# Linear attention for the sample tokens: states as the moving operand in four column groups, updates from stacked high and low parts

## The chip, the cores and the metric

The kernel runs on one core of a Trainium2 chip. The metric is the time of one execution on the device, in microseconds (us); the time before is the median of three runs. Profiles come from one further execution, recorded by the hardware profiler, and their times count from the start of the span.

## What is computed

The reference is one step of a two-layer decoder trunk for two groups of requests that share the weights: a prompt of 1024 tokens and 8 sample sequences of 8 tokens each. The first layer mixes with gated linear attention (4 heads, key width 128, value width 256), the second with sliding-window attention; each has a squared-ReLU MLP and a per-layer input embedding. The change is in the linear attention, and there in the sample sequences alone. Cut to that part, for one head:

```python
def step(state, inp):                    # a chunk: all 8 tokens of each sample sequence
    qc, kc, vc, lc = inp
    bc = jnp.cumsum(lc, axis=-2)         # log decay per token and key column
    ...
    o = einsum('bhij,bhje->bhie', attn, vc) + einsum('bhid,bhde->bhie', qc * exp(bc), state)
    last = bc[:, :, -1:, :]
    new_state = exp(last)[..., None] * state + einsum('bhjd,bhje->bhde', kc * exp(last - bc), vc)
```

For each of the 8 sequences b and each head there is a state of 128 x 256 numbers (`state_gla`). The output is the attention within the 8 tokens plus the decayed queries times the state; the new state is the decayed old one plus an outer product of the 8 tokens' keys and values.

## The kernel before, in words

Activations lie with the 1024 model columns in 8 groups of 128 partitions and all 1088 tokens (1024 prompt, then 64 sample) along the free dimension. Nearly all work is matrix products with weights, done in three matmuls: operands are split into a high part in the F32R type and a low part, and `mm3` (L163 to L165) adds high x high, high x low and low x high into one PSUM tile. Weight tiles are loaded on the SyncE queue (`load`, L77; all loads are kept in order), split by ScalarE (L139) and VectorE (L140), and used from a ring of 5 with 2 raw buffers.

The linear-attention layer (`gla_layer`) walks through the 4 heads. For each head `gla_steps` makes 9 steps: 8 chunks of 128 prompt tokens (c = 0 to 7) and one step (c = 8) for the 64 sample tokens. A step computes decays (`gla_lg`, `gla_pre`), scores by levels (`gla_scores`: one matmul a level, L524), and outputs (`gla_out`, or `gla_out_sample` for the samples). Between its pieces the driver in `gla_layer` (L322 to L334) puts the next head's projection (`gla_proj`) or, for the last head, gate products (`gla_gates`), metered by estimated cost. The order of the instructions on each engine is drawn up when the kernel is built, by priority and by estimated readiness, so pieces that stand later in the code can come earlier on an engine. PSUM tiles come from three rings: `mm` (3), `gs` (2) and `gx` (3).

In `gla_out_sample` (L566 to L591) the scores of the step lie in `pp` and `pd`, the 64 decayed keys transposed to tokens x key columns in `kt`, the decayed queries in `qe` (128 x 64), the decays of the states in `sm`, the sample tokens' values in `vs` (64 of 128 rows used, the rest zero). For each sequence b:

- `km` (L574, for two sequences at a time): `kt` masked to the 8 rows of b by `bmask`;
- the state is loaded into `s0` (a ring of 2, so the load of b waits until the state of b - 2 has been stored);
- L581: two matmuls, one for each half of the value columns, with 128 state columns as the stationary operand and the 8 queries of b as the moving one, so that 8 columns of `pi` come out for each;
- L583: one F32 matmul with `km` stationary and `vs` moving (256 columns) into `pu`;
- L584: VectorE makes the new state in place, and L585 stores it on the SyncE queue.

After the loop L588 makes the part within the sequences, ScalarE copies it out (L590) and VectorE adds `pi` (L591). `onorm` then normalises the head's outputs.

In the trace an instruction with F32 operands on TensorE has two weight loads and two matmul records (L581: 64 instructions, 128 records), called passes below; one with F32R operands has one of each.

Of the kernel before, what the change touches and what calls it, by code (L numbers as in the profile page):

```python
# [11 lines left out]
F32 = mybir.dt.float32  # L12
F32R = mybir.dt.float32r
U8 = mybir.dt.uint8
AF = mybir.ActivationFunctionType
ALU = mybir.AluOpType
# [3 lines left out]
P = 128  # L20
D = 1024
KT = D // P
SEQ = 1024
NB, NT = 8, 8
TS = NB * NT
# [6 lines left out]
DV = 256  # L32
# [6 lines left out]
R = (slice(0, 64), slice(64, 128))  # L39


def _dims(ap, dims):

    return bass.AP(tensor=ap.tensor, offset=ap.offset, ap=[list(ap.ap[0])] + [list(d) for d in dims])


class Trunk:
# [204 lines left out]
    def gla_layer(self):  # L252
        nc, I, O = self.nc, self.I, self.O
        with ExitStack() as ctx:
            ga = ctx.enter_context(self.tc.tile_pool(name="ga", bufs=1))
# [3 lines left out]
            for k in range(KT):  # L259
# [14 lines left out]
                if k == KT - 1:  # L274
                    for c0, cn in CH:
                        c = slice(c0, c0 + cn)
# [7 lines left out]
            self.load(self.wa2[:17], I["wa2"].rearrange("h r c -> r h c"))  # L284

            self.vs = ga.tile([P, DV], F32, name="vs")
            self.km = ga.tile([P, 2, P], F32, name="km")
            nc.gpsimd.memset(self.vs, 0.0)
            nc.gpsimd.memset(self.km, 0.0)
            tri = ga.tile([P, P], F32R, name="tri")  # L290
            tris = ga.tile([TS, TS], F32R, name="tris")
            tf = ga.tile([P, P], F32, tag="c128", name="tf", bufs=8)
# [7 lines left out]
            t = ga.tile([P, len(LV), P], F32, tag="E", name="masks", bufs=2).rearrange("p a b -> p (a b)")  # L300
# [2 lines left out]
            self.load(t[:TS, n:n + ns], I["msks"])  # L303
            nc.scalar.copy(msk, t[:, :n])
            nc.scalar.copy(msks, t[:TS, n:n + ns])
            bmask = ga.tile([TS, NB], F32, name="bmask")
            self.load(bmask, I["bmask"])
            og = ga.tile([P, 2], F32, name="og")
            self.load(og, I["ogain"])
            self.g = dict(tri=tri, tris=tris, msk=msk, msks=msks, bmask=bmask, og=og)  # L310
# [29 lines left out]
            o = [t for d in self.head for t in d["o"]]  # L340

            xs = []
            for k in range(KT):
                d = self.double("G3" if k < 4 else "G1")
# [166 lines left out]
    def gla_scores(self, h, c, pre):  # L511

        nc = self.nc
        E, ke, qe, sm = pre
        sample = c == 8
        w, levels = (TS, LVS) if sample else (P, LV)
        tok, qk, hw = c * P, self.head[h]["qk"], w // 2
        base = qk[:, 0, tok:tok + w]
        pp, pd = self.ps("gx"), self.ps("gx")
        for l, s in enumerate(levels):  # L520
            ev = E[:, l, :].rearrange("p (n two s) -> p n two s", two=2, s=s)
            nc.vector.tensor_tensor(ev, ev, _dims(base, ([2 * s, w // (2 * s)], [T + s, 2], [1, s])), op=ALU.mult)
            m = w - s if w - s > 64 else w
            nc.tensor.matmul(pp[:m, l * hw:(l + 1) * hw], lhsT=E[:, l, :m], rhs=ev[:, :, 1, :], start=True, stop=True)  # L524
        nc.vector.tensor_tensor(ke[:, :w], ke[:, :w], base, op=ALU.mult)
        nc.tensor.matmul(pd[:w, :w], lhsT=base, rhs=qk[:, 1, tok:tok + w], start=True, stop=True)
        nc.tensor.transpose(pd[:w, P:2 * P], in_=ke[:, :w], identity=self.ident)
        kt = self.c128("kt")
        nc.scalar.copy(kt[:w, :], pd[:w, P:2 * P])
        if c:  # L530
            nc.vector.tensor_tensor(qe[:, :w], qe[:, :w], qk[:, 1, tok:tok + w], op=ALU.mult)
        return pp, pd, kt, qe, sm
# [33 lines left out]
    def gla_out_sample(self, h, st):  # L566
        nc, ga, g, d = self.nc, self.ga, self.g, self.head[h]
        pp, pd, kt, qe, sm = st
        vs, km, o, tok = self.vs, self.km, d["o"], SEQ
        self.gla_pick(self.ats[:TS], g["msks"], pp, pd, TS, LVS)  # L570
        pi = self.ps("gx")
        for b in range(NB):
            if b % 2 == 0:
                nc.vector.tensor_tensor(km[:TS], kt[:TS, :].unsqueeze(1).broadcast_to([TS, 2, P]),  # L574
                                        g["bmask"][:, b:b + 2].unsqueeze(2).broadcast_to([TS, 2, P]), op=ALU.mult)
                pu = self.ps("gs")
            i = b % 2
            s0 = ga.tile([P, DV], F32, tag="s0", name=self.uid("s0"), bufs=2)
            self.load(s0, self.I["st0"][b, h])
            for e in range(2):  # L580
                nc.tensor.matmul(pi[:, e * TS + b * NT:e * TS + (b + 1) * NT], lhsT=s0[:, e * P:(e + 1) * P],  # L581
                                 rhs=qe[:, b * NT:(b + 1) * NT], start=True, stop=True)
            nc.tensor.matmul(pu[:, i * DV:(i + 1) * DV], lhsT=km[:, i, :], rhs=vs, start=True, stop=True)  # L583
            nc.vector.scalar_tensor_tensor(s0, s0, sm[:, b:b + 1], pu[:, i * DV:(i + 1) * DV], op0=ALU.mult, op1=ALU.add)  # L584
            nc.sync.dma_start(self.O["sts"][b, h], s0)  # L585
        po = self.ps("gx")
        for e in range(2):
            nc.tensor.matmul(po[:, e * TS:(e + 1) * TS], lhsT=vs[:, e * P:(e + 1) * P], rhs=self.ats, start=True, stop=True)  # L588
        for e in range(2):
            nc.scalar.copy(o[e][:, tok:tok + TS], po[:, e * TS:(e + 1) * TS])  # L590
            nc.vector.tensor_tensor(o[e][:, tok:tok + TS], o[e][:, tok:tok + TS], pi[:, e * TS:(e + 1) * TS], op=ALU.add)  # L591

    def onorm(self, o):
        nc, g = self.nc, self.g
# [644 lines left out]
```

## Time and profile before

| | |
|---|---|
| median of 3 runs | 2753.29 us (2752.90 to 2753.79) |
| profiled execution, its own time | 2754.8 us |
| its span | 2753.0 us |
| TensorE (PE) busy | 2720.5 us, 99% of the span |
| VectorE (DVE) busy | 1446.2 us, 53% |
| ScalarE (ACT) busy | 1057.7 us, 38% |
| sample steps of the four heads (first to last L581) | 148.8 to 449.9 us |

PE is the matmul side of TensorE and PEld its weight loads, which overlap PE. Matmuls are pipelined: the duration of one (331 ns for 362 columns) is longer than the distance from its start to the next one's start, so costs on PE are read from distances of starts. In a timeline row "x4" the first number is the start of the first of four, the second the time from there to the end of the last. In a row that groups instructions the number after the bar is busy time, then the mean in ns, then the idle time ahead of them and what ended it.

### The profile page before, as it was taken

Reading aid. Unit: us, or ns where it says so; the run is one execution under the profiler, and the core shown is the slowest. Engines: PE = TensorE matmul, PEld = TensorE weight load, DVE = VectorE, ACT = ScalarE, POOL = GpSimd, SP = SyncE. Lnnn points to the kernel's source line nnn. Section 1 sums busy time; section 2 is a strip of 40 time slices with the busy share of each in tenths; the row PEclk is TensorE's granted clock in tenths of the full one; section 3 lists DMA queues with packets and bytes.
Section 4 is the critical chain, followed back from the end, with each engine's and each line's share of the span. In section 5 each row is a group of like instructions: output and inputs, shape, how many; then the busy total and the mean of one; then the engine's idle time right before and its main releaser. Section 6 shows DMA issues by size and latency. Waiting matters only on the chain.

```text
span 2753.0 us, 43316 instructions
## 1 busy us (share of the span) xinstructions
PE 2720.5 (99%) x17265; PEld 2657.6 (97%) x17265; DVE 1446.2 (53%) x3481; ACT 1057.7 (38%) x2303; POOL 128.0 (5%) x155
## 2 busy tenths in 40 slices
PE   9999999999999999999999999999999999999997
PEld 8999999999999999999999888899999999999997
DVE  5767887443433343344755677654343333333687
ACT  5555566341221122123534666532221221222465
POOL 0000000001000000000000333200000000000000
PEclk9999999999999999999999999999999999999999
DMA  3021012321211111121122211221111111111153
GB/s 124 28 64 53 28 57 69 95 68 41 69 47 50 53 51 49 45 85 47 55 79 63 60 35 40 65 75 43 46 51 46 44 54 43 46 44 46 34 182 100
DMA packets 92704, 163.34 MB, mean 59 GB/s; under 512 B 11479, under 2 KB 30571, under 8 KB 92470
## 3 DMA queue, kind: packets, MB, share of 16 engines
q1 hardware_dynamic: 89557, 155.20, 18.6%
q10 hardware_dynamic: 1152, 4.46, 0.5%
q8 instruction: 136, 2.23, 0.3%
q0 software_dynamic: 1792, 0.92, 0.2%
q14 instruction: 67, 0.54, 0.1%
HBM read 145.94 MB, written 19.98 MB: 60 GB/s over the span
## 4 chain that ended last, share of the span: by engine, by line
PE 95%; DVE 2%; ACT 1%; DMA 1%; issue 0%; POOL 0%; DVEq 0%; SPq 0%; ACTq 0%; POOLq 0%
PE mm L163 21%; PE mm L164 21%; PE mm L165 21%; PE gx L165 7%; PE gx L164 7%; PE gx L163 7%; PE gx L524 2%; PE gx L1012 1%; PE gx L998 1%; PE gx L553 1%; PE gx L548 1%; PE gs L583 1%; PE gs L981 1%; PE gx L555 0%; PE gs L231 0%
## 5 line engine op out<-in xcount | busy, mean ns | idle before, releaser
L163 PE MATMUL mm<-G,whi 128*128 128x362 f32 (+1 forms) x3416 | 1128.8, 331 | 6.4 <-ACT G L195 6.0
L164 PE MATMUL mm<-G,whi 128*128 128x362 f32 (+1 forms) x3416 | 1127.6, 330 | 0.0
L165 PE MATMUL mm<-G,wlo 128*128 128x362 f32 (+1 forms) x3416 | 1127.3, 330 | 0.1
L163 PEld LDWEIGHTS mm<-G,whi 128*128 128x128 f32 x3416 | 642.1, 188 | 12.9 <-ACT G L195 6.4
L164 PEld LDWEIGHTS mm<-G,whi 128*128 128x128 f32 x3416 | 642.6, 188 | 3.9 <-issue 1.7
L165 PEld LDWEIGHTS mm<-G,wlo 128*128 128x128 f32 x3416 | 642.2, 188 | 3.4 <-issue 1.2
L139 ACT CAST whi<-raw 128x512 fp32r<-128x512 f32 (+1 forms) x368 | 226.4, 619 | 657.0 <-PE mm L164 618.5
L165 PE MATMUL gx<-G,wlo 128*128 128x362 f32 (+1 forms) x1048 | 344.2, 328 | 0.0
L164 PE MATMUL gx<-G,whi 128*128 128x362 f32 (+1 forms) x1048 | 343.8, 328 | 0.0
L163 PE MATMUL gx<-G,whi 128*128 128x362 f32 (+1 forms) x1048 | 343.1, 328 | 0.0
L140 DVE TENSOR_TENSOR wlo<-raw,whi 128x512 fp32r<-128x512 f32 (+1 forms) x368 | 251.9, 691 | 67.7 <-ACT whi L139 67.0
L692 DVE TENSOR_TENSOR H<-H,mm 128x364 f32<-128x364 f32 (+1 forms) x256 | 136.2, 532 | 277.2 <-PE mm L165 276.0
L681 ACT ACTIVATE tmp<-tmp 128x362 f32<-128x362 f32 (+1 forms) x192 | 97.2, 507 | 462.5 <-DVE tmp L680 457.1
L165 PEld LDWEIGHTS gx<-G,wlo 128*128 128x128 f32 x1048 | 198.0, 189 | 0.0
L163 PEld LDWEIGHTS gx<-G,whi 128*128 128x128 f32 x1048 | 197.9, 189 | 0.0
L164 PEld LDWEIGHTS gx<-G,whi 128*128 128x128 f32 x1048 | 197.7, 189 | 0.0
L683 DVE TENSOR_TENSOR G<-tmp,G 128x362 fp32r<-128x362 f32 (+1 forms) x192 | 102.9, 537 | 157.5 <-ACT G L682 157.2
L680 DVE SCALAR_TENSOR_TENSOR tmp<-mm,rb 128x364 f32<-128x364 f32 (+1 forms) x128 | 68.6, 536 | 196.4 <-PE mm L165 196.4
L692 DVE TENSOR_TENSOR H<-H,gx 128x362 f32<-128x362 f32 x128 | 68.0, 532 | 141.7 <-PE gx L165 141.7
L225 ACT ACTIVATE tmp<-H 128x362 f32<-128x362 f32 (+1 forms) x126 | 63.6, 506 | 132.6 <-DVE H L629 74.2
L682 ACT CAST G<-tmp 128x362 fp32r<-128x362 f32 (+1 forms) x192 | 95.1, 496 | 5.8
L226 DVE TENSOR_TENSOR acc<-acc,tmp 128x362 f32<-128x362 f32 (+1 forms) x126 | 67.2, 535 | 36.2 <-ACT tmp L225 35.3
(244 smaller groups left out, 3024.5 us busy)
## 6 DMA issues: line engine op xcount, KB each, us to landing
raw<-in_w_up SPq DMA_DIRECT2D x128, 256.0 KB, 2.6
raw<-in_w_down SPq DMA_DIRECT2D x128, 256.0 KB, 2.6
G<-in_w_gate SPq DMA_DIRECT2D x24, 512.0 KB, 3.9
raw<-in_w_o SPq DMA_DIRECT2D x32, 256.0 KB, 2.9
raw<-in_w_q SPq DMA_DIRECT2D x24, 256.0 KB, 3.3
x<-in_xT ACTq DMA_DIRECT2D x8, 544.0 KB
hd<-H SPq DMA_DIRECT2D x8, 544.0 KB, 2.6
x<-hd SPq DMA_DIRECT2D x8, 544.0 KB, 3.6
```

Of the source, the lines that this page charges most:

```text
L139: nc.scalar.copy(hi[:, s], raw[:, s])
L140: nc.vector.tensor_tensor(lo[:, s], raw[:, s], hi[:, s].bitcast(F32), op=ALU.subtract)
L163: mm(out, lhsT=w[0], rhs=x[0], start=first, stop=False)
L164: mm(out, lhsT=w[0], rhs=x[1], start=False, stop=False)
L165: mm(out, lhsT=w[1], rhs=x[0], start=False, stop=last)
L225: nc.scalar.activation(sq[:, :cn], h[:, s], AF.Square)
L226: nc.vector.tensor_tensor(self.acc[:, s], self.acc[:, s], sq[:, :cn], op=ALU.add)
L680: nc.vector.scalar_tensor_tensor(t[:, :cn], ps, 0.0, rb[:, s], op0=ALU.max, op1=ALU.mult)
L681: nc.scalar.activation(t[:, :cn], t[:, :cn], AF.Square)
L682: nc.scalar.copy(u[:, 0, s], t[:, :cn])
L683: nc.vector.tensor_tensor(u[:, 1, s], t[:, :cn], u[:, 0, s].bitcast(F32), op=ALU.subtract)
L692: nc.vector.tensor_tensor(h[:, s], h[:, s], ps, op=ALU.add)
```

## The change

- The state is no longer the stationary operand. For each sequence the 32 query columns of its group of four (`qe[:, half*32:half*32+32]`) are stationary, and the state's 256 columns stream past them; the result goes to partitions 32i to 32i+31 of `pi`, i = b mod 4, and columns 0 to 255 or 256 to 511 for the first and the last four sequences. Of the 32 rows of each result only the 8 of sequence b are used. So there are 8 F32 matmuls for each head, on four column groups of the array, in place of 16.
- `pi` now has tokens in its partitions. ScalarE copies its two halves out (`it`), four transposes on TensorE turn them back (`pt`, a further `gx` tile), and the addition at the end picks each sequence's 8 columns.
- The update of the state uses F32R: values and keys are split into high and low parts; `k2` has the high parts of the keys in rows 0 to 63 and the low parts in rows 64 to 127, `v2[:, 0]` the high part of the values in both halves of the rows, `v2[:, 1]` their low part in both. Two F32R matmuls (`km[:, b]` against `v2[:, 0]`, then `v2[:, 1]`) take the place of one F32 matmul. `km` holds all 8 sequences, masked in one VectorE instruction; the mask `bmask` is loaded into both halves of the rows.
- `s0` has a ring of 8 instead of 2, and the 8 loads stand at the head of the function.
- In `gla_scores`, at the prompt chunks, the level s = 64 takes 65 columns of the stationary operand instead of 128 (`max(w - s, 65)`); the other levels and the sample step are as before.

```diff
@@ -284,9 +284,7 @@
             self.load(self.wa2[:17], I["wa2"].rearrange("h r c -> r h c"))
 
             self.vs = ga.tile([P, DV], F32, name="vs")
-            self.km = ga.tile([P, 2, P], F32, name="km")
             nc.gpsimd.memset(self.vs, 0.0)
-            nc.gpsimd.memset(self.km, 0.0)
             tri = ga.tile([P, P], F32R, name="tri")
             tris = ga.tile([TS, TS], F32R, name="tris")
             tf = ga.tile([P, P], F32, tag="c128", name="tf", bufs=8)
@@ -303,8 +301,9 @@
             self.load(t[:TS, n:n + ns], I["msks"])
             nc.scalar.copy(msk, t[:, :n])
             nc.scalar.copy(msks, t[:TS, n:n + ns])
-            bmask = ga.tile([TS, NB], F32, name="bmask")
-            self.load(bmask, I["bmask"])
+            bmask = ga.tile([P, NB], F32, name="bmask")
+            for r in R:
+                self.load(bmask[r], I["bmask"])
             og = ga.tile([P, 2], F32, name="og")
             self.load(og, I["ogain"])
             self.g = dict(tri=tri, tris=tris, msk=msk, msks=msks, bmask=bmask, og=og)
@@ -520,7 +519,7 @@
         for l, s in enumerate(levels):
             ev = E[:, l, :].rearrange("p (n two s) -> p n two s", two=2, s=s)
             nc.vector.tensor_tensor(ev, ev, _dims(base, ([2 * s, w // (2 * s)], [T + s, 2], [1, s])), op=ALU.mult)
-            m = w - s if w - s > 64 else w
+            m = w if sample else max(w - s, 65)
             nc.tensor.matmul(pp[:m, l * hw:(l + 1) * hw], lhsT=E[:, l, :m], rhs=ev[:, :, 1, :], start=True, stop=True)
         nc.vector.tensor_tensor(ke[:, :w], ke[:, :w], base, op=ALU.mult)
         nc.tensor.matmul(pd[:w, :w], lhsT=base, rhs=qk[:, 1, tok:tok + w], start=True, stop=True)
     def gla_out_sample(self, h, st):
         nc, ga, g, d = self.nc, self.ga, self.g, self.head[h]
         pp, pd, kt, qe, sm = st
-        vs, km, o, tok = self.vs, self.km, d["o"], SEQ
+        vs, o, tok = self.vs, d["o"], SEQ
+        s0 = []
+        for b in range(NB):
+            s0.append(ga.tile([P, DV], F32, tag="s0", name=self.uid("s0"), bufs=NB))
+            self.load(s0[b], self.I["st0"][b, h])
+
+        v2 = ga.tile([P, 2, DV], F32R, tag="v2", name=self.uid("v2"), bufs=1)
+        k2 = self.c128("k2").bitcast(F32R)
+        nc.scalar.copy(v2[R[0], 0, :], vs[R[0]])
+        nc.scalar.copy(v2[R[1], 0, :], vs[R[0]])
+        nc.scalar.copy(k2[R[0]], kt[R[0], :])
+        for r in R:
+            nc.vector.tensor_tensor(v2[r, 1, :], vs[R[0]], v2[R[0], 0, :].bitcast(F32), op=ALU.subtract)
+        nc.vector.tensor_tensor(k2[R[1]], kt[R[0], :], k2[R[0]].bitcast(F32), op=ALU.subtract)
         self.gla_pick(self.ats[:TS], g["msks"], pp, pd, TS, LVS)
+
         pi = self.ps("gx")
         for b in range(NB):
+            i, half = b % 4, b // 4
+            nc.tensor.matmul(pi[32 * i:32 * i + 32, half * DV:(half + 1) * DV], lhsT=qe[:, half * 32:half * 32 + 32],
+                             rhs=s0[b], start=True, stop=True)
+        it = [self.t364() for _ in range(2)]
+        for half in range(2):
+            nc.scalar.copy(it[half][:, :DV], pi[:, half * DV:(half + 1) * DV])
+        km = ga.tile([P, NB, P], F32R, tag="km", name=self.uid("km"), bufs=1)
+        nc.vector.tensor_tensor(km, k2.bitcast(F32).unsqueeze(1).broadcast_to([P, NB, P]),
+                                g["bmask"].unsqueeze(2).broadcast_to([P, NB, P]), op=ALU.mult)
+        for b in range(NB):
             if b % 2 == 0:
-                nc.vector.tensor_tensor(km[:TS], kt[:TS, :].unsqueeze(1).broadcast_to([TS, 2, P]),
-                                        g["bmask"][:, b:b + 2].unsqueeze(2).broadcast_to([TS, 2, P]), op=ALU.mult)
                 pu = self.ps("gs")
-            i = b % 2
-            s0 = ga.tile([P, DV], F32, tag="s0", name=self.uid("s0"), bufs=2)
-            self.load(s0, self.I["st0"][b, h])
-            for e in range(2):
-                nc.tensor.matmul(pi[:, e * TS + b * NT:e * TS + (b + 1) * NT], lhsT=s0[:, e * P:(e + 1) * P],
-                                 rhs=qe[:, b * NT:(b + 1) * NT], start=True, stop=True)
-            nc.tensor.matmul(pu[:, i * DV:(i + 1) * DV], lhsT=km[:, i, :], rhs=vs, start=True, stop=True)
-            nc.vector.scalar_tensor_tensor(s0, s0, sm[:, b:b + 1], pu[:, i * DV:(i + 1) * DV], op0=ALU.mult, op1=ALU.add)
-            nc.sync.dma_start(self.O["sts"][b, h], s0)
-        po = self.ps("gx")
+            out = pu[:, (b % 2) * DV:(b % 2 + 1) * DV]
+            for i in range(2):
+                nc.tensor.matmul(out, lhsT=km[:, b, :], rhs=v2[:, i, :], start=(i == 0), stop=(i == 1))
+            nc.vector.scalar_tensor_tensor(s0[b], s0[b], sm[:, b:b + 1], out, op0=ALU.mult, op1=ALU.add)
+            nc.sync.dma_start(self.O["sts"][b, h], s0[b])
+        po, pt = self.ps("gx"), self.ps("gx")
         for e in range(2):
             nc.tensor.matmul(po[:, e * TS:(e + 1) * TS], lhsT=vs[:, e * P:(e + 1) * P], rhs=self.ats, start=True, stop=True)
         for e in range(2):
+            for half in range(2):
+                c = (e * 2 + half) * P
+                nc.tensor.transpose(pt[:, c:c + P], in_=it[half][:, e * P:(e + 1) * P], identity=self.ident)
+        for e in range(2):
             nc.scalar.copy(o[e][:, tok:tok + TS], po[:, e * TS:(e + 1) * TS])
-            nc.vector.tensor_tensor(o[e][:, tok:tok + TS], o[e][:, tok:tok + TS], pi[:, e * TS:(e + 1) * TS], op=ALU.add)
+            dst = o[e][:, tok:tok + TS].rearrange("p (a b t) -> p a b t", a=2, b=4)
+            src = _dims(pt[:, e * 2 * P:], ([P, 2], [32 + NT, 4], [1, NT]))
+            nc.vector.tensor_tensor(dst, dst, src, op=ALU.add)
```

## Prediction

> **What bounds the kernel now.** I read the page first (busy time, slices, chain), then busy time by stretch around the linear attention, then the waits, then the order of time around one sample step.
>
> ```profile
> span 2753.0 us, 43316 instructions
> PE 2720.5 (99%) x17265; PEld 2657.6 (97%) x17265; DVE 1446.2 (53%) x3481; ACT 1057.7 (38%) x2303; POOL 128.0 (5%) x155
> PEclk9999999999999999999999999999999999999999
> PE 95%; DVE 2%; ACT 1%; DMA 1%; issue 0%; POOL 0%; DVEq 0%; SPq 0%; ACTq 0%; POOLq 0%
> ```
>
> PE is busy 99% of the span at its full granted clock, and the chain that ended last is 95% PE. That is an average; what counts is the stage that is changed. Busy time there:
>
> ```profile
> 146.00:480.00 334.00, 332.29 (x2335) 317.69 (x2334) 255.32 (x878) 195.23 (x470) 2.84 (x5) 1.00 0.18 55
> 175.00:235.00 60.00, 59.72 (x464) 57.14 (x463) 50.35 (x205) 39.77 (x114) 0.00 (x0) 1.00 0.11 32
> 235.00:270.00 35.00, 35.00 (x241) 33.85 (x240) 23.33 (x72) 13.03 (x34) 0.00 (x0) 1.00 0.28 87
> ```
>
> The columns are stretch, length, then busy time of PE, PEld, DVE, ACT and POOL. From the first sample step to the end of the layer PE is idle for 334.00 - 332.29 = 1.7 us; DVE has 255 of 334 us. In 235 to 270, around the second head's sample step, PE has no gap at all and DVE is busy for 67%. So time taken off PE here should come off the end, as long as no other chain takes its place. The waits say the same:
>
> ```profile
> PE gx L581 <- DMA s<-in_st: 0.7, 1, 0.7
> PEld gx L581 <- DMA s<-in_st: 1.2, 2, 1.0
> DVE s L584 <- PE gx L581: 18.8, 12, 3.7
> ```
>
> The two-deep ring of states makes DVE wait 18.8 us for L581, and the step drags on; PE itself waits for states only 0.7 + 1.2 us, because other matmuls are put between. A deeper ring by itself is worth no more than that. What counts is the PE time of the instructions.
>
> **What goes from PE.** One pair of sequences in the second head's sample step, matmuls and then weight loads, and the counts:
>
> ```profile
> 240.98 0.51 PE L581 MATMUL gx<-qe,s 128*128 128x8 f32 x4
> 241.34 0.68 PE L583 MATMUL gs<-vs,km 128*128 128x256 f32 x2
> 241.86 0.51 PE L581 MATMUL gx<-qe,s 128*128 128x8 f32 x4
> ...
> 240.86 0.53 PEld L581 LDWEIGHTS gx<-qe,s 128*128 128x128 f32 x4
> ...
> L581 PEld LDWEIGHTS gx<-qe,s x128: 186/191/192, 148.8 to 449.9; 128*128 128x128 f32 x128
> L581 PE MATMUL gx<-qe,s x128: 170/256/277, 148.9 to 449.9; 128*128 128x8 f32 x128
> L583 PE MATMUL gs<-vs,km x64: 377/378/462, 149.2 to 449.1; 128*128 128x256 f32 x64
> ```
>
> Four weight loads of L581 take 0.53 us in all and the last 0.19, so they start (0.53 - 0.19) / 3 = 0.113 us apart: with 8 moving columns a pass costs its weight load. From the first L581 to the next sequence's L581 are 0.88 us for four such passes and two of L583, so L583 costs (0.88 - 4 x 0.113) / 2 = 0.214 a pass. L581 in all: 128 x 0.113 = 14.5 us. L583: 64 x 0.214 = 13.7 us. Both go.
>
> The 65 columns at level s = 64 of the prompt chunks:
>
> ```profile
> L524 PE MATMUL gx<-E 128*128 128x64 f32 x64 | 12.1, 271 | 0.0
> L524 PEld LDWEIGHTS gx<-E x472: 132/188/196, 75.3 to 427.4; 128*127 128x127 f32 x22, 128*120 128x120 f32 x22, 128*128 128x128 f32 x22, 128*126 128x126 f32 x21
> 237.73 0.42 PEld L524 LDWEIGHTS gx<-E 128*64 128x64 f32 x6
> ```
>
> 64 passes have 128 stationary columns and 64 moving ones. At 64 stationary columns six loads start (0.42 - 0.13) / 5 = 0.058 us apart. I take 0.058 for 65 columns, half of 0.113 as the columns are. Saved: 64 x (0.113 - 0.058) = 3.5 us. The bounds are 0 (the load isn't what limits it) and 3.5.
>
> **What comes to PE.** The update in F32R, 8 x 2 x 4 = 64 passes with 256 moving columns. The same shape in the value projection, the first and the last of 15 in a row:
>
> ```profile
> 142.57 0.27 PE L163 MATMUL mm<-whi,G 128*128 128x256 f32 x1
> ...
> 144.23 0.28 PE L165 MATMUL mm<-whi,G 128*128 128x256 f32 x1
> ```
>
> That is 1.66 / 14 = 0.119 us a pass, and 64 x 0.119 = 7.6 us.
>
> The states as moving operand: 8 F32 matmuls a head with 32 stationary and 256 moving columns, 16 passes. The kernel has four column groups of 32 elsewhere, in the sample tokens' window attention:
>
> ```profile
> 1626.85 1.09 PE L998 MATMUL gx<-ident,S 128*128 128x128 f32 x8
> 1627.87 0.42 PE L1031 MATMUL gs<-kp,qs 64*32 64x128 f32 x8
> 1628.22 0.43 PE L1033 MATMUL gs<-Ks,qs 64*128 64x64 f32 x2
> L998 PE MATMUL gx<-ident,S 128*128 128x128 f32 x240 | 38.8, 287 | 4.2 <-DVE S L963 3.1 <-POOL S L963 0.3
> ```
>
> Eight passes of 128 columns in four groups start and end within 0.42 us; one after the other their columns alone would take 8 x 0.107 (half of L583's pass). So four run side by side. The last L998 starts at 1626.85 + 1.09 - 0.29 = 1627.65, the next full-width instruction at 1628.22: 0.57 us, less one L998 pass (0.114, below) and two rounds of 0.107, leaves 0.24 for going into the mode, spreading the groups, and coming out. A head then costs four rounds of 0.214 and 0.24, 1.1 us; the four heads 4.4 us.
>
> This is a drain on a change of mode, as the Trainium skill states it ("TensorEngine Tiling (Array Packing)", Key Properties); the rows agree, and give it the size of 0.24 us for the way in and out.
>
> What the rows don't show is four groups with 128 rows each: L1031 has 64. Bounds: side by side as in L1031 (4.4 us), or 16 passes in a row, 16 x 0.214 + 0.24 = 3.7 us a head, 14.7 us. I take the first, the nearest row in shape, and keep both.
>
> Transposes back, 4 a head of 128 columns: eight of L998 start (1.09 - 0.29) / 7 = 0.114 us apart; 16 x 0.114 = 1.8 us.
>
> The Trainium skill speaks against these ("TensorE: Matmul & The Clock Gate", Part 4): about 275 ns for a transpose in a kernel's context. By that they would take 16 x 0.275 = 4.4 us and the gain would be 2.6 us smaller, an estimate; the L998 row disagrees, since there 0.287 is the length of one and not its distance from the next.
>
> **The sum for PE.** Off: 14.5 + 13.7 + 3.5 = 31.7. On: 7.6 + 4.4 + 1.8 = 13.8. Net 17.9 us less.
>
> **What the other engines get.** The rows for their new work:
>
> ```profile
> L574 DVE TENSOR_TENSOR km<-kt,bmask 64x256 f32<-64x256 f32 x16 | 6.6, 414 | 5.1 <-PE gs L583 4.3 <-ACT kt L529 0.8
> L193 DVE TENSOR_TENSOR G<-H,G 128x1088 fp32r<-128x1088 f32 x22 | 28.1, 1288 | 9.4 <-ACT G L192 9.3
> L525 DVE TENSOR_TENSOR ke<-ke,G 128x128 f32<-128x128 f32 x32 | 9.2, 286 | 0.0
> L466 ACT CAST lgh<-lge 128x256 fp32r<-128x256 f32 x16 | 6.3, 396 | 0.7 <-DVE lge L465 0.7
> L392 ACT ACTIVATE G<-mm,rt 128x256 f32<-128x256 f32 x32 | 15.1, 471 | 23.9 <-PE mm L165 23.7
> ```
>
> DVE, a head: `km` with 1024 columns 1024/1088 x 1.288 = 1.21, two differences for `v2` at 0.414, one for `k2` at 0.286, together 2.3 in place of 4 x 0.414 = 1.7: 0.6 us more. ACT: three copies for the splits at no more than 0.396 and two of `pi` at 0.471, 2.1 us more. In 235 to 270 DVE has 11.7 us free and ACT 22, so I cost both at nothing. Without that cover the way from `kt` to the first update is what shows: a copy of at most 0.396, a difference of 0.286 and 1.21 for the mask, 1.9 us, against 0.414 before, 1.5 us a head.
>
> Behind it on the in-order PE queue stand that head's updates and whatever the build put after them; behind the long `km` on DVE the next head's score products. The extra `gx` tile and the new order of stores get no price of their own; a rival takes the first. The loads:
>
> ```profile
> 109.82 0.90 SPq L77 DMA_DIRECT2D s<-in_st  x2
> DMA to landing us min/median/max: 2.0/2.3/2.8
> L77 SPq DMA_DIRECT2D s<-in_st x32: 333/366/426, 109.8 to 446.3; - x32
> ```
>
> SP issued the first two states at 109.8, 39 us before the first L581 (148.8). Now all eight can go then, 8 x 0.43 = 3.4 us of queue, with weight loads behind them. A weight tile feeds 36 matmuls of 362 columns, over 36 x 0.119 = 4.3 us, and three are kept ahead, so I cost this at nothing; uncovered it is 3.4 us a head. The second small load of `bmask` lies ahead of the sample steps: nothing.
>
> **From the span to the time.** 2753.0 - 17.9 = 2735.1 for the span. The profiled execution took 2754.8, 1.8 more than its span and 1.5 more than the median of the three runs. So 2735.1 + 1.8 - 1.5 = 2735.4 against a median of 2753.29. A measurement of this kernel tells some 0.2%, 5.5 us, from no change.
>
> **The rivals.**
>
> - *PE waits at each sample step*, for the split and the mask (1.5 us a head) or for weights (up to 3.4): 4 x 1.5 = 6.0 gives 2741.4; up to 2749.0 for the weights. For: DVE's queue is a shared one. Against: PE waits for DVE hardly at all now, with DVE slower to its first update than PE could be. 0.13.
> - *The groups run in a row, or at half speed*, since four streams of 128 rows are read at once. Half speed costs 4 x 4 x 0.214 = 3.4, 2738.8; in a row 14.7 - 4.4 = 10.3, 2745.7. Against: L1031's rows. 0.12, mostly for half speed.
> - *The visits are split* (the one without a measurable gain). If the eight matmuls of a head are placed one by one between other work, as each state lands, each costs two passes and the change of mode, 2 x 0.214 + 0.24 = 0.67; 32 of them are 21.4 in place of 4.4, and 0.9 us of gain is left: 2752.4. For: the build does put other matmuls between L581 now. Against: it does so because of the ring of two; with eight buffers the states can be there 39 us early. 0.04. The drain named above is what makes this dear.
> - *Slower: the next head's first step starves.* `po` and `pt` take two of the three `gx` tiles until the last additions, and the next step's `pp` and `pd` need two. If that step waits, and with it the chain of DVE work behind it, PE works off the projections and then stands idle for up to a step. A step is (240.98 - 148.8) / 9 = 10.2 us; at three joints 30.7, so 2735.4 + 30.7 = 2766.1. It decides from (17.9 + 5.5) / 3 = 7.8 us a joint. Against: now `pi` alone holds a tile through the whole loop, and PE loses 1.7 us in 334. 0.03.
> - *The 65 columns bring nothing*: 2738.9. Against: the 0.058 above. 0.03.
>
> **How the numbers follow.** The forecast, all terms within a microsecond or two, has 0.65; the rivals 0.35. Faster by over 0.2% needs a time below 2747.8: the forecast, the columns, the groups, and nearly all of the waits, 0.92. Within 0.2%: the split visits and the rest, 0.05. Slower: 0.03. The range goes down by the idle 1.7 us and as much again for the drains (2732) and up to the waits at 1.5 us a head (2741.4), which takes in half speed and the columns: 2732 to 2742. In it lie the forecast, half of the waits, half speed and the columns, about 0.84.
>
> **What would show it.** Right: L581's line as 64 passes of 128*32, four starting within some 0.02 us and the rounds 0.21 apart, one visit a head; L583's line as 64 passes 0.12 apart; L524 without 128*128 at the prompt chunks but with 128*65, loads 0.06 apart; PE still without gaps from 146 to the end of the layer, and that end some 18 us earlier. Wrong: rounds 0.4 apart or more (half speed), several visits a head, PE idle for over 1 us ahead of an update or of the next head's scores, or a later stage that takes longer than before.

## The result, and the profile after

| | before | after |
|---|---|---|
| median | 2753.54 us (4 runs, 2752.90 to 2754.47) | 2739.61 us (4 runs, 2738.03 to 2741.02) |
| ratio | | 0.9948, 95% interval 0.9936 to 0.9959 |
| profiled execution, its own time | 2754.8 us | 2741.02 us |
| its span | 2753.0 us | 2738.9 us |

The change takes off 13.9 us by the medians and 14.1 by the spans. The forecast was 17.9. The lines shift: the level matmuls are now L523 (524 before), `gla_out`'s L552 and L554 (553 and 555); in `gla_out_sample` the states are L587, the updates L600, the transposes L609.

The page of the kernel after, the same rows as those shown of before:

```profile
span 2738.9 us, 43239 instructions
PE 2706.5 (99%) x17217; PEld 2639.3 (96%) x17217; DVE 1448.5 (53%) x3481; ACT 1065.8 (39%) x2326; POOL 128.0 (5%) x154
PEclk9999999999999999999999999999999999999999
PE 96%; DVE 2%; ACT 1%; issue 0%; DMA 0%; POOL 0%; DVEq 0%; SPq 0%; ACTq 0%; POOLq 0%
```

PE is busy 14.0 us less (2720.5 - 2706.5), and the span is 14.1 shorter: PE was the bound and still is.

Busy time by stretch, after (stretch, length, then PE, PEld, DVE, ACT, POOL, then the granted clock):

```profile
146.00:480.00 334.00, 332.14 (x2369) 313.67 (x2368) 265.42 (x885) 210.40 (x499) 2.84 (x5) 1.00 0.19 59
235.00:270.00 35.00, 34.96 (x241) 32.19 (x234) 32.63 (x105) 22.11 (x57) 0.00 (x0) 1.00 0.24 76
```

PE is as full as before. DVE went from 23.33 to 32.63 of the 35 us around the second sample step, ACT from 13.03 to 22.11. Most of that is work that now falls into this stretch: in the whole kernel DVE is busy only 2.3 us more (1448.5 against 1446.2) and ACT 8.1, of which 3.8 are three further loads of function tables (below). The cover under which the new work was costed at nothing is nearly used up there (2.4 us are left on DVE), but it held.

The order of time around the first sample step, and the groups of its new lines (duration min/median/max, first and last start):

```profile
147.39 0.28 PE L165 MATMUL mm<-whi,G 128*64 128x256 f32 x1
147.60 1.07 PE L587 MATMUL gx<-s,qe 128*32 128x256 f32 x16
148.60 0.32 PE L605 MATMUL gx<-ats,vs 128*128 128x64 f32 x1
```

```profile
L587 PEld LDWEIGHTS gx<-s,qe x64: 106/110/111, 147.6 to 409.6; 128*32 128x32 f32 x64
L587 PE MATMUL gx<-s,qe x64: 378/379/404, 147.6 to 409.8; 128*32 128x256 f32 x64
...
L600 PE MATMUL gs<-v,km x64: 277/282/388, 150.1 to 418.6; 128*128 128x256 f32 x64
```

All 16 passes of a head are one visit (a run of small matmuls between two of the projections) of 148.60 - 147.60 = 1.0 us, and so in all four heads. In the records they start four at a time within 0.02 us, the rounds at 147.60, 147.84, 148.06 and 148.27.

To place the difference I put the matmuls of L163 to L165 in order of their starts, the same 14,544 in both kernels, and compare the times of those with the same number. From the 400th (about 74 us) to the 2000th (about the end of the linear attention) the kernel before takes 400.9 us and the kernel after 385.8. This stretch is called the stage below. From there to the 8000th both take 1004.4 us. In the next thousand, the window attention, after takes 330.8 and before 329.3. So the stage gave 15.1 us, and 1.5 were lost where nothing was changed. That loss shows as clock:

The window attention by stretch, before:

```profile
1708.00:1712.00 4.00, 3.94 (x26) 3.65 (x26) 4.00 (x15) 2.14 (x11) 0.99 (x1) 1.00 0.00 0
...
1726.00:1734.00 8.00, 7.74 (x63) 6.09 (x59) 5.42 (x26) 4.11 (x16) 1.78 (x2) 0.70 0.00 0
```

The same, after:

```profile
1708.00:1712.00 4.00, 3.43 (x26) 2.86 (x25) 3.23 (x16) 1.39 (x4) 1.04 (x1) 0.61 0.00 2
...
1719.00:1726.00 7.00, 6.90 (x45) 5.28 (x47) 3.74 (x17) 3.14 (x10) 0.98 (x1) 0.51 0.00 0
```

The granted clock halves for pieces of 3.4 us: 6.8 us in all before (from 1724.0), 3.4 and 6.8 after (from 1708.8 and 1719.1). One piece costs up to 1.7 us, as passes then take about twice as long. The Trainium skill ("TensorE: Matmul & The Clock Gate", Part 1) tells of free-running windows of 3413 ns after which the clock is set to full or half; the pieces in these traces, 3.4 us or twice that, agree.

So the stage itself fell short of the forecast by 2.8 us (17.9 - 15.1). There is a candidate for that. The waits of PE in the linear attention, after, and its order of time at the longest:

```profile
PE gx L552 <- DVE at L540: 1.8, 3, 1.4
PE gx L523 <- DVE E L521: 0.2, 1, 0.2
```

```profile
391.39 0.32 PE L165 MATMUL mm<-G,wlo 128*128 128x362 f32 x1
393.09 0.49 PE L552 MATMUL gx<-at,G 128*128 128x128 f32 x2 [1.38 <-DVE at L540]
```

From start to start that is 1.70 us in place of 0.165. ScalarE in the time before it, after:

```profile
383.12 1.28 ACT L416 ACT_TABLE_LOAD   x1
...
386.73 1.28 ACT L463 ACT_TABLE_LOAD   x1
388.03 0.31 ACT L463 ACTIVATE lge<-lge 64x128 f32<-64x128 f32 x1
388.24 0.19 ACT L502 ACTIVATE sm<-bc 128x1 f32<-128x1 f32 x1
388.45 1.28 ACT L503 ACT_TABLE_LOAD   x1
389.74 0.20 ACT L503 ACTIVATE sm<-bc 128x1 f32<-128x1 f32 x1
389.96 1.28 ACT L107 ACT_TABLE_LOAD   x1
391.26 0.95 ACT L491 ACTIVATE E<-E 128x896 f32<-128x896 f32 x1
392.11 0.39 ACT L504 ACTIVATE ke<-bc,sm 128x128 f32<-128x128 f32 x1
```

In the order that the build drew up for the changed kernel, L463 and L503 stand between the Silu of L416 and the preload at L107. So the whole kernel has 28 table loads in place of 25, and `ke` is late. Against this candidate: the kernel before has waits too, only spread out. Its list for the stage adds up to 1.8 us (0.7 for a state, 0.4, 0.3, 0.2, 0.2), that of after to 2.0.

### The profile page after: what moved, and what is told of

Same layout as the page of the kernel before. It is cut to its first block, busy times and chain, and to the rows that moved or that the text cites. A ratio compares the mean times of both kernels' runs of the same rounds, so it can differ in the third digit from the quotient of the medians.

```text
span 2738.9 us, 43239 instructions
## 1 busy us (share of the span) xinstructions
PE 2706.5 (99%) x17217; PEld 2639.3 (96%) x17217; DVE 1448.5 (53%) x3481; ACT 1065.8 (39%) x2326; POOL 128.0 (5%) x154
## 4 chain that ended last, share of the span: by engine, by line
PE 96%; DVE 2%; ACT 1%; issue 0%; DMA 0%; POOL 0%; DVEq 0%; SPq 0%; ACTq 0%; POOLq 0%
PE mm L163 22%; PE mm L164 22%; PE mm L165 22%; PE gx L165 7%; PE gx L164 7%; PE gx L163 7%; PE gx L523 2%; PE gx L1035 1%; PE gx L1021 1%; PE gx L552 1%; PE gx L547 1%; PE gs L1004 1%; PE gs L231 0%; PE gx L554 0%; PE gs L1005 0%
## 5 line engine op out<-in xcount | busy, mean ns | idle before, releaser
L163 PE MATMUL mm<-G,whi 128*128 128x362 f32 (+1 forms) x3416 | 1129.3, 331 | 6.2 <-ACT G L195 6.2
L165 PE MATMUL mm<-G,wlo 128*128 128x362 f32 (+1 forms) x3416 | 1127.7, 330 | 0.1
L163 PEld LDWEIGHTS mm<-G,whi 128*128 128x128 f32 x3416 | 642.9, 188 | 12.7 <-ACT G L195 6.6
L165 PEld LDWEIGHTS mm<-G,wlo 128*128 128x128 f32 x3416 | 642.6, 188 | 3.2 <-issue 1.6
L165 PE MATMUL gx<-G,wlo 128*128 128x362 f32 (+1 forms) x1048 | 344.3, 329 | 0.0
L163 PE MATMUL gx<-G,whi 128*128 128x362 f32 (+1 forms) x1048 | 343.1, 328 | 0.0
L165 PEld LDWEIGHTS gx<-G,wlo 128*128 128x128 f32 x1048 | 198.0, 189 | 0.0
L163 PEld LDWEIGHTS gx<-G,whi 128*128 128x128 f32 x1048 | 197.8, 189 | 0.0
```

Of the source, the lines that this page charges most:

```text
L163: mm(out, lhsT=w[0], rhs=x[0], start=first, stop=False)
L165: mm(out, lhsT=w[1], rhs=x[0], start=False, stop=last)
```

## The theories

**First theory.** The passes cost what the forecast says and they add; what is missing went to waits and halved clocks, which come from the order of instructions that each build draws up. **Rival.** One of the terms is mis-sized (the column groups, the update or the 65 columns), and the parts done alone show which.

## Experiments

The numbers of all of them first. "Stage" is the stretch defined above, "waits" the sum of PE's waits in it that the profile lists, "half clock" the time in it at a granted clock of 0.5, all in the profiled execution. "Rest" is the stage less the waits and less half of the half clock, so about the passes alone.

| kernel | median us | ratio to before, 95% interval | stage | waits | half clock | rest |
|---|---|---|---|---|---|---|
| before | 2754.0 | | 400.9 | 1.8 | 0 | 399.1 |
| after, again (r_after) | 2740.13 | 0.9946 (0.9932 to 0.9959) | 385.8 | 2.0 | 0 | 383.8 |
| p1_cols | 2751.13 | 0.9985 (0.9976 to 0.9994) | 397.4 | 1.5 | 0 | 395.9 |
| p2_ring | 2762.55 | 1.0033 (1.0020 to 1.0045) | 409.0 | 2.2 | 13.6 | 400.0 |
| p3_groups | 2751.00 | 0.9986 (0.9977 to 0.9995) | 397.4 | 3.1 | 0 | 394.3 |
| p4_update | 2763.25 | 1.0029 (1.0018 to 1.0040) | 410.6 | 8.2 | 13.6 | 395.6 |
| q_apart | 2757.72 | 1.0009 (1.0000 to 1.0018) | 402.2 | 0.7 | 0 | 401.5 |
| q_serial | 2739.93 | 0.9943 (0.9931 to 0.9956) | 385.9 | 2.0 | 0 | 383.9 |
| q_table | 2737.88 | 0.9940 (0.9928 to 0.9953) | 385.7 | 1.1 | 0 | 384.6 |
| u_cols | 2742.12 | 0.9957 (0.9945 to 0.9969) | 388.4 | 2.1 | 0 | 386.3 |
| u_groups | 2756.30 | 1.0009 (1.0001 to 1.0017) | 406.0 | 2.8 | 27.2 | 389.6 |
| u_update | 2748.21 | 0.9980 (0.9971 to 0.9989) | 395.5 | 2.9 | 3.4 | 390.9 |

### One part alone, on the kernel before

p1_cols: the 65 columns only.

```diff
-            m = w - s if w - s > 64 else w
+            m = w if sample else max(w - s, 65)
```

> The kernel before with the 65 columns at level s = 64 alone. Theory A (each part is worth the TensorE passes that it saves, less what TensorE waits in the order that this build gives it; a half-clock window of 3.4 us more or less moves a run by 1.5 us): 64 weight loads from 0.113 to 0.058 us apart, 3.5 us less, so about 2750.0 against 2753.5, and the linear-attention stage shorter by 3.5 us. Theory B (the sum of 17.9 us was short because a term was mis-sized): if it is this term, no change within 1 us.

The stage went from 400.9 to 397.4, the 3.5 us forecast. Single runs lie between 2746.81 and 2753.92; the profiled one, 2746.81, has a full clock all through the window attention (the stretch 1719 to 1726 has 1.00), which explains its place at the low end.

p2_ring: the ring of eight and the loads ahead, nothing else.

```diff
+        s0 = []
+        for b in range(NB):
+            s0.append(ga.tile([P, DV], F32, tag="s0", name=self.uid("s0"), bufs=NB))
+            self.load(s0[b], self.I["st0"][b, h])
...
-            s0 = ga.tile([P, DV], F32, tag="s0", name=self.uid("s0"), bufs=2)
-            self.load(s0, self.I["st0"][b, h])
```

> The kernel before with eight buffers for the states and the eight loads at the head of the function, nothing else. Theory A: TensorE waited 1.9 us for states in all, so 0 to 1.9 us less, 2751.6 to 2753.5; VectorE's wait of 18.8 us for L581 shrinks to a few us, and the sample step of a head takes under 12 us in place of 24, with no gain from that. Theory B: as the step is shortened by over 10 us a head, some of that shows, over 4 us less.

It is 8.6 us slower. The order of time on PE in p2_ring (its state matmuls are L583, its updates L585), then two stretches of it:

```profile
150.17 3.19 PE L583 MATMUL gx<-qe,s 128*128 128x8 f32 x28
153.22 0.64 PE L590 MATMUL gx<-ats,vs 128*128 128x64 f32 x4
...
155.46 0.51 PE L163 MATMUL mm<-G,whi 128*128 128x364 f32 x1
155.76 0.50 PE L164 MATMUL mm<-G,whi 128*128 128x364 f32 x1
...
431.92 3.63 PE L583 MATMUL gx<-qe,s 128*128 128x8 f32 x32
435.40 0.41 PE L164 MATMUL mm<-G,whi 128*128 128x364 f32 x1
```

```profile
150.00:153.90 3.90, 3.90 (x35) 3.87 (x34) 0.73 (x3) 0.96 (x2) 0.00 (x0) 0.99 0.57 168
153.90:157.30 3.40, 3.40 (x11) 3.12 (x11) 1.79 (x7) 2.19 (x5) 0.00 (x0) 0.51 0.11 39
```

With all eight states at hand, 28 passes of 8 moving columns run back to back. PE reads as busy for 3.90 of 3.90 us and PEld for 3.87. Then the clock is halved: passes of 364 columns start 0.30 apart in place of 0.165, and 3.4 us hold 11 matmul records in place of 28 (the same stretch of before). This comes at three of the four heads, 13.6 us in all, worth up to 6.8. The fourth head has 32 such passes in a row, from 431.92, and the clock stayed at full behind them; what sets it apart is not shown.

p3_groups: the ring, the column groups and the transposes; update and 128 columns as before.

```diff
         pi = self.ps("gx")
         for b in range(NB):
+            i, half = b % 4, b // 4
+            nc.tensor.matmul(pi[32 * i:32 * i + 32, half * DV:(half + 1) * DV], lhsT=qe[:, half * 32:half * 32 + 32],
+                             rhs=s0[b], start=True, stop=True)
+        it = [self.t364() for _ in range(2)]
+        for half in range(2):
+            nc.scalar.copy(it[half][:, :DV], pi[:, half * DV:(half + 1) * DV])
```

> The kernel before with the ring of eight, the states as moving operand in four column groups, and the transposes back; update and levels as before. Theory A: 14.5 off, 4.4 and 1.8 on, 8.3 us less, 2745.2, up to 1.9 lower with the waits for states gone. Theory B: if the groups are the mis-sized term, 4 us less or under, 2749.5 or more.

Only 3.0 us by the medians, 4.8 in the rest, where the passes alone give 14.5 - 4.4 - 1.8 = 8.3: the median is where the rival put it. No half clock in the stage, but a wait that is 0.2 us at the longest in the kernel before and that the kernel after does not have:

```profile
PE gs L481 <- ACT lgh L466: 2.0, 2, 1.8
```

Here too it stands behind table loads on ScalarE (five of 1.28 us between 350 and 360 us; 29 in the kernel).

p4_update: the stacked update in F32R only, with the ring of two.

```diff
+        km = ga.tile([P, NB, P], F32R, tag="km", name=self.uid("km"), bufs=1)
...
-            nc.tensor.matmul(pu[:, i * DV:(i + 1) * DV], lhsT=km[:, i, :], rhs=vs, start=True, stop=True)
+            for i in range(2):
+                nc.tensor.matmul(out, lhsT=km[:, b, :], rhs=v2[:, i, :], start=(i == 0), stop=(i == 1))
```

> The kernel before with the update in stacked high and low parts alone; ring of two and stationary states as before. Theory A: 13.7 off and 7.6 on, 6.1 us less, 2747.4. Theory B: if the update is the mis-sized term, because its longer chain on ScalarE and VectorE holds up TensorE, 3 us less or under, 2750.5 or more, with waits ahead of L583's successor of 0.5 us or more a head.

It is 9.3 us slower though its passes are 6.1 us cheaper. The waits of PE in p4_update, and its clock behind one of them:

```profile
PE mm L163 <- ACT whi L139: 2.8, 2, 1.8
PE gx L589 <- DMA s<-in_st: 2.6, 4, 1.4
PE gs L593 <- DVE s L594: 1.8, 2, 1.3
```

```profile
358.00:361.00 3.00, 0.96 (x7) 0.77 (x7) 2.33 (x6) 2.75 (x7) 0.00 (x0) 0.93 0.74 205
361.00:364.00 3.00, 2.68 (x9) 2.42 (x9) 2.87 (x7) 0.88 (x2) 0.00 (x0) 0.50 0.18 64
```

8.2 us of waits with the small ones, and 13.6 us at half clock, 6.8 from 360.6 and 6.8 from 463.0, both beside idle times of 1.3 to 1.8 us. The parts alone sum to 2.8 + 3.0 - 9.3 = -3.5, a loss; the whole gains 14. So a part alone does not size a term. In the rest they give 3.2, 4.8 and 3.5 us, 11.5 together, against 15.3 of the whole by the same measure and 17.9 by the forecast: less than forecast for each, which speaks for the rival, though no one term stands out.

### What the halved clock needs

q_apart: p2_ring, with the state matmuls of a sequence ordered behind the update of the one before.

```diff
+                if b:
+                    self.order(r.ins, mu.ins)
-            nc.tensor.matmul(pu[:, i * DV:(i + 1) * DV], lhsT=km[:, i, :], rhs=vs, start=True, stop=True)
+            mu = nc.tensor.matmul(pu[:, i * DV:(i + 1) * DV], lhsT=km[:, i, :], rhs=vs, start=True, stop=True)
```

> The kernel with only the ring of eight states and the loads ahead, with one thing more: the state matmuls of a sequence wait for the update matmul of the sequence before it, so that they don't run back to back. No work is left out. If the 8.6 us that the ring alone cost come from the run of weight loads with 8 moving columns each, after which the granted clock is halved for 3.4 to 6.8 us, there is no stretch at half clock in the sample steps of the linear attention and the kernel falls back to 2754 to 2757 us, within 3 us of the kernel before. If they come from waits and table loads of the other build order, it stays at 2760 to 2763 us.

The same stretch as in p2_ring, in q_apart:

```profile
153.90:157.30 3.40, 3.40 (x31) 3.29 (x29) 2.89 (x10) 0.00 (x0) 0.00 (x0) 1.00 0.25 86
```

No half clock in any sample step, and the stage falls from 409.0 to 402.2: 6.8 us, half of the 13.6. The median, 2757.72, is 0.7 us above the range expected and 3.7 above before; of that the stage holds 1.3. So the halving in the sample steps hangs on the run of passes with 8 columns; the matmuls are the same in number and shape. That a run is not always enough, p2_ring's fourth head shows.

### One part undone, on the kernel after

u_cols: 128 columns again (p1_cols' edit, reversed).

> The changed kernel with one part undone: the level s = 64 takes 128 columns again. If the terms of the forecast add once the rest is in place, the linear attention takes 3.5 us more (385.8 to 389.3 us between the two marks used for the stage) and the kernel 2743.6 us. If each build's own order of instructions moves the time by as much as a part is worth, the stage comes out anywhere from 386 to 393 us, with the difference in idle time of TensorE or in how the small matmuls are split up between the projections.

The stage grew by 2.6 us, the rest by 2.5 and the median by 2.0 (against 2740.13), where 3.5 were expected. PE's wait ahead of L552 is there as in after.

u_groups: the states stationary again, no transposes; ring, stacked update and 65 columns stay.

```diff
-            i, half = b % 4, b // 4
-            nc.tensor.matmul(pi[32 * i:32 * i + 32, half * DV:(half + 1) * DV], lhsT=qe[:, half * 32:half * 32 + 32],
-                             rhs=s0[b], start=True, stop=True)
...
+            for e in range(2):
+                nc.tensor.matmul(pi[:, e * TS + b * NT:e * TS + (b + 1) * NT], lhsT=s0[b][:, e * P:(e + 1) * P],
+                                 rhs=qe[:, b * NT:(b + 1) * NT], start=True, stop=True)
```

> The changed kernel with one part undone: the states are the stationary operand again, 16 F32 matmuls of 8 moving columns a head and no transposes; ring of eight, stacked update and 65 columns stay. By the passes alone 14.5 less 4.4 less 1.8, 8.3 us more (stage 394.1, kernel 2748.4). If a run of weight loads with 8 moving columns each halves the granted clock after it, as with the ring alone, there are stretches at half clock of 3.4 to 6.8 us behind the sample steps, and up to 1.7 us more for each 3.4 us of them: stage 396 to 402, kernel 2750 to 2757. If that halving belonged to something else in the ring's build, no such stretch shows in the sample steps and the stage is at 394 to 395.

16.2 us slower than after, and 2.3 slower than before. PE around the first sample step of u_groups, and the stretch behind:

```profile
148.70 3.63 PE L587 MATMUL gx<-qe,s 128*128 128x8 f32 x32
152.19 0.64 PE L602 MATMUL gx<-ats,vs 128*128 128x64 f32 x4
...
153.89 0.51 PE L163 MATMUL mm<-G,whi 128*128 128x364 f32 x1
```

```profile
153.90:157.30 3.40, 3.40 (x17) 3.40 (x17) 1.36 (x4) 1.64 (x6) 0.00 (x0) 0.55 0.12 39
```

Half clock behind all four sample steps (20.4 us), and 6.8 us more behind PE's wait of 2.4 us for ScalarE (L480, to 365.7). The stage, 406.0, lies above the 396 to 402 expected. The rest is 5.8 us over after's, where the passes alone give 8.3. So of 20.2 us of stage most is clock, up to 13.6. The profiled execution is the slowest of twelve (2762.52), but the clock shows in the others too: the one with a mean granted clock of 0.996, as before the change, took 2749.37, near the 2748.4 of the passes alone, and the other eleven, at 0.991 to 0.994, took 2755.60 to 2762.52. In the whole change the column groups are worth twice what their passes say.

u_update: the single F32 update again; ring, groups and 65 columns stay.

```diff
-            for i in range(2):
-                nc.tensor.matmul(out, lhsT=km[:, b, :], rhs=v2[:, i, :], start=(i == 0), stop=(i == 1))
+            nc.tensor.matmul(pu[:, i * DV:(i + 1) * DV], lhsT=km[:, i, :], rhs=vs, start=True, stop=True)
```

> The changed kernel with one part undone: the update of the states is one F32 matmul of 256 columns against km of 64 rows again, with km masked for two sequences at a time; ring of eight, column groups and 65 columns stay. By the passes alone 13.7 less 7.6, 6.1 us more (stage 391.9, kernel 2746.2). The same kernel without the 65 columns had its stage at 397.4, so 393.9 if the columns add. If the stage lies between 391 and 394.5 the terms hold to some 2 us; further off, the build's own order weighs as much as the part.

8.1 us slower than after, the stage 9.7 longer and 1.0 above the range expected. It has 3.4 us at half clock, behind PE's longest wait:

```profile
355.00:359.50 4.50, 2.67 (x18) 2.37 (x17) 3.31 (x12) 4.29 (x11) 0.00 (x0) 0.99 0.00 0
359.50:362.90 3.40, 3.40 (x14) 3.40 (x13) 2.58 (x11) 3.34 (x7) 0.00 (x0) 0.51 0.01 2
```

The rest is 7.1 us over after's, against 6.1 by the passes. p3_groups and u_update differ by the 65 columns alone and have the same wait ahead of L481: 394.3 - 390.9 = 3.4. Behind that wait the clock stayed at full in p3_groups.

So from the top the terms are 2.5 of 3.5 (u_cols), 5.8 of 8.3 and 7.1 of 6.1, 15.4 of 17.9 together: what the whole gave. The mechanism of the first theory, waits and half clocks, explains most of what p4_update and u_groups are off by; of the 5.3 us that p3_groups is off it covers 1.3. For the whole's missing 2.8 us it falls: after has no more waits than before (2.0 us against 1.8) and no half clock in the stage. There the rival is nearer. The states' matmuls fall shortest, 4.8 from below and 5.8 from above where 8.3 were worked out; but the rest of each build also holds what its order of instructions makes of the other passes, so the parts do not settle which price was off; the stages of before and after, shared out among their passes, say more (below).

### The column groups and the table loads

q_serial: the sequences in the order 0, 4, 1, 5, 2, 6, 3, 7, so that two matmuls of one group follow each other.

```diff
-        for b in range(NB):
+        for b in (0, 4, 1, 5, 2, 6, 3, 7):
             i, half = b % 4, b // 4
```

> The changed kernel, but the eight sequences are built in the order 0, 4, 1, 5, 2, 6, 3, 7, so that two matmuls of the same column group follow each other. No work is left out. If a column group's second pass holds up the other groups behind it (the queue is strictly in order), a head of sample tokens takes some 13 rounds of 0.22 us in place of four: 9 times 0.215 us more, 1.9 us a head, 7.7 us for four heads (about 2747). If the four groups take their passes from the queue independently, as the first profile hints where the first passes of all four groups start ahead of every second pass, four rounds stay and the time is the changed kernel's within 0.5 us.

The first sample step of q_serial:

```profile
147.88 1.09 PE L587 MATMUL gx<-s,qe 128*32 128x256 f32 x16
148.90 0.66 PE L605 MATMUL gx<-ats,vs 128*128 128x64 f32 x4
```

1.02 us against 1.00, four rounds, in all four heads, and the stage unchanged at 385.9. The built program does hold the two matmuls of a group next to each other on PE. Passes of a group that is free start ahead of earlier ones that wait for a group that is busy. The Trainium skill says that matmuls stay in program order and only weight loads are pulled ahead ("TensorE: Matmul & The Clock Gate", Part 2); for passes on different column groups the runs disagree, as 16 passes in this order would need some 13 rounds.

r_after: the kernel after, once more.

> The changed kernel once more. The first theory (passes add as forecast, part of it is lost to waits of the new build order and to 3.4 us stretches at half clock that fall into the window attention in some executions) expects a median of 2739.6 us within 1.5, the linear attention up to its last matmul at 385 to 386 us again, the 1.7 us gap of TensorE near 391 us again since it comes from the order of the instructions, and single runs that differ by multiples of some 1.5 to 2 us. The rival (the 1.7 us gap and the half clock stretches of the first profile are chance) expects that the gap is gone in the second profile and the median nearer to 2736.

The stage is 385.8 us again and the wait at L552 is there again, now 392.84 us after the span's start. It belongs to the order of the instructions. The window attention took 329.3 us, as before the change, and the profiled execution 2738.2 us; so the 1.5 us there come and go from one execution to the next. The median stayed at 2740.13.

q_table: the Exp and Ln of the layer ordered behind the table preload, each Silu behind the last of them.

```diff
+    def tabled(self, r):
+        if getattr(self, "lastpre", None) is not None:
+            self.order(r.ins, self.lastpre)
+        self.lastexp = r.ins
+        return r
...
+            self.order(self.lastsilu.ins, self.lastexp)
...
-            nc.scalar.activation(sm[:, 0:1], bc[:, P - 1:P], AF.Exp, scale=1.0 / 16)
+            self.tabled(nc.scalar.activation(sm[:, 0:1], bc[:, P - 1:P], AF.Exp, scale=1.0 / 16))
```

> The changed kernel with one thing more: on ScalarE each Exp and Ln of the linear attention comes after the table preload ahead of it, and each Silu after the last of them, so that the 28 table loads become 25 as in the kernel before. No work is left out. If the three loads of 1.28 us between a Silu and the preload are what delays ke and starves TensorE at 391 us, the 1.7 us gap there goes and the kernel takes 1.4 to 1.7 us less than the changed kernel (about 2738.0). If the gap belongs to something else (VectorE's splits ahead of it), the loads go and the time stays within 0.5 us of the changed kernel. If the added order makes ScalarE late elsewhere, it is slower by 1 us or more.

The 28 loads became 25, and of PE's waits between 380 and 400 us only this is left in q_table:

```profile
PE gx L555 <- ACT kt L536: 0.2, 1, 0.2
```

So the table loads did make the wait. But the stage is 385.7 us, no shorter than in after: the rest grew by as much as the waits fell. The small matmuls lie differently there (they interrupt the projections 167 times in place of 162); that the gain was spent in this is likely and not shown. The median of 2737.88 is lower, but the five runs (2736.19 to 2741.25) overlap with those of r_after (2738.20 to 2740.76); no gain is shown, and no kernel tried is shown to beat the kernel after.

## Why the prediction was right, and where it was off

The time lies in the range and on the side that had 0.92. By its steps:

- **PE bounds the stage, so its time comes off the end.** Right: 14.0 us less busy time, 14.1 us less span, and the matmuls behind the stage keep their distances.
- **Column groups on.** Right: one visit a head, rounds of about 0.22 us, 1.0 us a visit against 1.1. Groups with 128 rows run side by side at the full rate, which the rows of before did not show. Half speed and groups in a row are out.
- **L581 and L583 off.** This is where the sum was too large. The 0.113 and 0.214 us were read from one pair of sequences in which L581 and L583 follow each other; elsewhere they lie between projections. The stage can be shared out whole: to each pass the distance from its start to the next start, less idle time. By this L581 has 11.9 us and L583 11.0 in the kernel before, 22.9 in place of 28.2. Where each distance is charged to the later pass instead, they have 27.4. So the term was 1 to 5 us too large; neighbours share the rest, and no run here parts it further.
- **F32R and transposes on.** By the first way of sharing, the updates have 8.6 us in the kernel after, the groups 4.0 and the transposes 1.3: 13.9 in place of 13.8 (15.8 by the second way). In the order of time three transposes start within 0.22 us, 0.11 apart. Each of the 16 has one record, not two, and it lasts 0.272 us, near the 275 ns that the Trainium skill states ("TensorE: Matmul & The Clock Gate", Part 4); that is the length of one and not its price here.
- **A part that no term had.** Off, on and 3.5 us for the levels make 12.5 of the 15.1 us by the first way. The other 2.6 are 2.9 less in passes that the change does not touch, 2.4 of it in the projections (254.9 us before, 252.5 after), and 0.3 more idle time. By the second way the projections lose 2.5. Why they became cheaper is open. So that the sum came so near the measured time is luck in part: a price that was too high, and a gain that nobody had worked out.
- **The 65 columns.** 3.5 in the stage when done alone, 2.6 when undone from the whole, against the 3.5 worked out.
- **"I cost both at nothing".** Held in sum: the waits of PE are 2.0 us against 1.8. Their place is new. The rival of PE waiting came true not at the update of a sample step but ahead of a prompt chunk's outputs (L552), through table loads that no term had, and the waits for states are gone.
- **"A deeper ring by itself is worth no more than that."** Wrong in sign: alone it cost 8.6 us, mostly since it lets weight loads run in a row and the clock is halved behind them (q_apart, without such runs, has 6.8 us less of stage). The change escapes because the column groups replace those passes; without them it would have been 2.3 us slower than the kernel before (u_groups).
- **From the span to the time.** Single executions move by some 3 us with the pieces at half clock in the window attention, which the working did not have. They are likely the other part of the 4.2 us between 2735.4 and 2739.61.

## What to carry to other kernels

Where one engine is 99% busy, a sum of its passes by distances of starts gave the side and most of the size here, with some luck; read the price of a pass at several places, since neighbours share it. Do not size the parts of a change by running each alone: here they sum to a loss of 3.5 us where the whole gains 14, as each build has its own waits. Before you give a kernel all its operands early, look at what will then run in a row on PE.

## What was not expected of the hardware

- 28 to 32 passes in a row with 128-column weight loads and 8 moving columns halved the granted clock for 3.4 or 6.8 us in seven of eight sample steps, although PE reads as 100% busy (p2_ring, u_groups); the same passes in runs of four never did (q_apart).
- An idle time of PE of about 1.8 us can do the same (p4_update, 1.79 us ahead of 361.32; u_update, 1.83 us ahead of 358.28), but does not always: 1.81 us in p3_groups, ahead of the same L481, and 1.38 us at 391 us in after left the clock at full.
- Matmuls on four column groups are started out of the order in which they were issued (q_serial).
